# State-space decay matrix from one row-spreading matmul per head and a clamped difference on ScalarE, in place of matmuls of products that POOL made

## The chip, the cores and the metric

The kernel runs on one core of one Trainium2 chip. The metric is device time in microseconds (us): the median of three runs, 1414.44 us before the change (1413.89 to 1421.01). Five engines work side by side, each through its own queue in program order: TensorE (PE in the profile, with its weight loads as PEld), VectorE (DVE), ScalarE (ACT), GpSimd (POOL) and SyncE (SP, which issues most transfers).

## What is computed

The reference is one layer of a hybrid network over 512 tokens of width 1024: an adaptive layer norm, three branches (attention, pooling, a state-space mixer), their gated sum, and a mixture of experts. The change touches the state-space branch alone, which has 32 heads in 4 groups. Cut to what matters:

```python
def ssd_mixer(z, xbc, dt_raw, ...):
    dt = jax.nn.softplus(dt_raw + dt_bias)            # per token and head
    a_cs = jnp.cumsum(dt * a, axis=2)                 # a < 0: running sum in a block
    seg = a_cs[:, :, :, None] - a_cs[:, :, None, :]   # difference of two tokens
    decay = jnp.where(causal, jnp.exp(jnp.where(causal, seg, 0.0)), 0.0)
    cb = jnp.einsum('bclgn,bcsgn->bclsg', cm, bm)     # per group, shared by its 8 heads
    scores = cb[..., None] * decay * dt[:, :, None]
    y_diag = jnp.einsum('bclsgr,bcsgrp->bclgrp', scores, xs)
    states = jnp.einsum('bcsgn,bcsgr,bcsgrp->bcgrpn', bm, decay_end * dt, xs)
    ...                                               # states carried from block to block
    y = y_diag + y_off + d_skip * xs
    y = y * jax.nn.silu(z)                            # then a group norm and w_ssm_o
```

Both kernels use blocks of 128 tokens, so 4 blocks (b = 0 to 3) for the 512 tokens.

## The kernel before

Weights are streamed from memory as 1 MB tiles. Each is split into a high and a low part of a faster matmul type (`whi` by a cast on ScalarE, line 84; the rest by a subtraction on VectorE, line 85, in place of the raw tile), and every product is made of three matmuls (lines 103 to 105, `mm3`). Through most of the kernel these matmuls fill TensorE.

The state-space branch (`ssd_branch`) takes its four groups g = 0 to 3 one after the other. `ssd_proj` makes a group's inputs by projection: x (two weight tiles, moving tiles 512 wide), B and C (`bmt`, `cmt`, one weight tile), then z (two weight tiles, eight result tiles `zs` of 24 matmuls, 256 wide). Each z tile leaves PSUM by a tanh on ScalarE (`zt`, line 463) and a product on VectorE (line 464); projections have four PSUM buffers (tag `mm`), so z tile 6 needs the buffer of z tile 2. Everything else shares four PSUM buffers of the tag `aux`.

`ssd_group` then goes through the 4 blocks. In each it makes C·B (line 480), which VectorE masks into `cbm` (line 482). In two halves of four heads POOL makes the products `rh` and `rl` of the lower triangle with a head's step (line 492), two matmuls with a strict triangle turn these into sums of steps between two tokens (lines 495 and 496), ScalarE takes the exponential (`sc`, line 498), VectorE multiplies with `cbm` (line 499), and only then can TensorE multiply the four heads' scores with the inputs `xdt` (line 502). `rh`, `rl` and `xdt` have one buffer each. Between blocks the state `st` is carried (lines 513 to 522). `ssm_out` (lines 545 to 556) projects the group before back to the model width with `yh` and `yl`; these matmuls, or the next group's, are what TensorE has between the steps of `ssd_group`. `decays` (lines 366 to 416) prepares the steps once, in group 0.

The order of instructions on each engine is made when the program is built: a scheduler places each instruction by program order as priority and by its own estimates of time. On the chip an engine takes its queue strictly in that order, and waits on semaphores for the others.

Of the kernel before, what the change touches and what calls it, by code (L numbers as in the profile page):

```python
# [30 lines left out]
C_ID, C_SEL, C_REC, C_KEY, C_G4, C_IE, C_IOB, C_PU, C_SGN, C_TA, C_TB, C_SLOT, C_K = 0, 128, 144, 208, 224, 228, 244, 251, 257, 258, 262, 266, 394  # L31
C_TRI, C_STR, C_BEF, C_MASK, C_N = 394, 522, 650, 778, 906
S_C, S_BADA, S_B48, S_ALOG, S_DSK, S_CW, S_CB, S_NW, S_PS, S_BR, S_N = 0, 8, 56, 57, 89, 121, 217, 241, 257, 265, 281
# [22 lines left out]
class Net:  # L56
# [88 lines left out]

    # ---------------------------------------------------------------- whole
    def build(self):
# [28 lines left out]
    def consts(self):  # L176
        nc, K = self.nc, self.K
        c = self.c = K.tile([P, C_K], F32, name="consts")
        e = self.ce = self.C.tile([P, C_N - C_K], F32, name="early")
        s = self.s = K.tile([P, S_N], F32, name="small")  # L180
        self.ident = c[:, C_ID:C_ID + P]
        self.tri, self.strict, self.before, self.mask = (e[:, i * P:(i + 1) * P] for i in range(4))
        self.mhalf = K.tile([P, NB], F32, name="mhalf")
# [9 lines left out]
    def copies(self):  # L193
        nc, K, c = self.nc, self.K, self.c
        self.ident_b = K.tile([P, P], BF16, name="ident_b")
        nc.vector.tensor_copy(self.ident_b, self.ident)
        self.mask_b = K.tile([P, P], BF16, name="mask_b")
        nc.vector.tensor_copy(self.mask_b, self.mask)
        self.ones_b = K.tile([P, P], BF16, name="ones_b")
        nc.vector.tensor_copy(self.ones_b, self.ones)  # L200
        self.bef_b = K.tile([P, P], BF16, name="bef_b")
        nc.vector.tensor_copy(self.bef_b, self.before)
        self.strict_r = self.C.tile([P, P], F32R, name="strict_r")
        nc.scalar.copy(self.strict_r, self.strict)
# [159 lines left out]

    # ---------------------------------------------------------------- dt, f
    def decays(self):
        nc, T, K, s, pz = self.nc, self.T, self.K, self.s, self.pz
        v = nc.vector
        n = NB * 48
        t = [T.tile([P, 512], F32, name=nm, tag=nm, bufs=1) for nm in ("y", "yo")]  # L370
        z, a = t[0][:, :n], t[0][:, n:2 * n]
# [45 lines left out]

    # ---------------------------------------------------------------- SSD
    def conv(self, ps, cc, out):
# [9 lines left out]
    def ssd_proj(self, g):  # L429
# [17 lines left out]
        wt = self.weights(self.I["wu"][5 * g + 2])  # L447
        bmt = T.tile([P, S], F32, name="bmt", tag="bmt", bufs=2)
        cmt = T.tile([P, S], F32, name="cmt", tag="cmt", bufs=2)
# [5 lines left out]
        bmn = T.tile([P, S], F32, name="bmn", tag="bmn", bufs=1)  # L455
        nc.scalar.activation(bmn, pt, AF.Copy, scale=0.5)
        zs = T.tile([P, NB, 512], F32, name="zs", tag="zs", bufs=1)
        for u in range(2):
            wt = self.weights(self.I["wu"][5 * g + 3 + u])
            for b in range(NB):  # L460
# [4 lines left out]
                                               op0=OP.add, op1=OP.mult)  # L465
        return xsn, bmt, cmt, bmn, zs

    def ssd_group(self, g, xsn, bmt, cmt, bmn, zs):
        nc, T, s = self.nc, self.T, self.s
# [7 lines left out]
        for b in range(NB):  # L477
            tb = slice(b * P, (b + 1) * P)
            pc = self.aux_tile()
            nc.tensor.matmul(pc[:, :P], bmt[:, tb], cmt[:, tb], start=True, stop=True)  # L480
            cbm = T.tile([P, P], F32, name="cbm", tag="cbm", bufs=2)
            v.tensor_tensor(cbm, pc[:, :P], self.tri4, OP.mult)
            xdt = T.tile([P, 512], F32, name="xdt", tag="xdt", bufs=1)
            v.tensor_tensor(h8(xdt[:, :]), h8(xsn[:, b]), b8(self.sp[:, b, 16 + g * 8:24 + g * 8]), OP.mult)
            py = self.aux_tile()
            for q in range(2):
                h4 = slice(g * 8 + q * 4, g * 8 + q * 4 + 4)
                tb4 = self.tri[:, None, :].to_broadcast([P, 4, P])
                rs = []
                for nm, src in (("rh", self.dah.bitcast(F32)), ("rl", self.dal)):  # L490
                    r = T.tile([P, 4, P], F32R, name=nm, tag=nm, bufs=1)
                    nc.gpsimd.tensor_tensor(r, tb4, src[:, b, h4][:, :, None].to_broadcast([P, 4, P]), OP.mult)  # L492
                    rs.append(r)
                pe = self.aux_tile()
# [8 lines left out]
            y = T.tile([P, 512], F32, name="y", tag="y", bufs=1)  # L503
            nc.gpsimd.tensor_tensor(h8(y[:, :]), h8(xsn[:, b]), b8(s[:, S_DSK + g * 8:S_DSK + g * 8 + 8]), OP.mult)  # L504
            v.tensor_tensor(y, py, y, OP.add)
            if b:
                po = self.aux_tile()
                nc.tensor.matmul(po, cmt[:, tb], state, start=True, stop=True)
                yo = T.tile([P, 512], F32, name="yo", tag="yo", bufs=1)
                v.tensor_tensor(h8(yo[:, :]), h8(po[:, :]), b8(self.ex[:, 0, b, hs]), OP.mult)  # L510
                v.tensor_tensor(y, y, yo, OP.add)
            if b < NB - 1:
                v.tensor_tensor(h8(xdt[:, :]), h8(xsn[:, b]), b8(self.dtd[:, b, hs]), OP.mult)
                pst = self.aux_tile()
                nc.tensor.matmul(pst, bmn[:, tb], xdt, start=True, stop=True)
# [6 lines left out]
                state = new  # L522
            v.tensor_tensor(yg[:, b], y, zs[:, b], OP.mult)
            nc.scalar.activation(y, yg[:, b], AF.Square, accum_out=ssq[:, b:b + 1])
# [61 lines left out]

    # ---------------------------------------------------------------- pool
    def pool_branch(self):
# [46 lines left out]

    # ---------------------------------------------------------------- attention
    def att_branch(self):
# [995 lines left out]
def _layout(inp):  # L1633
# [9 lines left out]
    c[:, C_BEF:C_BEF + P] = n[:, None] < n[None]  # L1643
    c[:, C_MASK:C_MASK + P] = np.where(n[None] > n[:, None], BIG, 0.0)
    c[:, C_SEL:C_SEL + H] = (n[:, None] % 32) == np.arange(H)[None]
    for i, w in enumerate((2, 4, 8, 16)):
# [83 lines left out]
```

## Time and profile before

| | before |
|---|---|
| device time, median of 3 (range) | 1414.44 us (1413.89 to 1421.01) |
| span of the profiled execution | 1413.1 us |
| mean granted TensorE clock | 0.958 |
| PE busy | 1299.2 us, 92% |
| PE weight loads busy | 1059.9 us, 75% |
| VectorE busy | 1075.4 us, 76% |
| ScalarE busy | 651.5 us, 46% |
| POOL busy | 394.3 us, 28% |

The page tells of one profiled execution, whose span is 1.3 us below the median of the timed runs. A busy share is an average over the whole kernel. A matmul's listed time is longer than its step, since matmuls are pipelined: what one costs in a full queue is the distance between two starts. The four groups of the state-space branch lie between 60 us and 480 us. In the tables by stretch, "PEclk" is the clock that the chip granted to TensorE: 1.00 is its upper level (2.4 GHz), 0.50 its lower (1.2 GHz).

### The profile page before, as it was taken

To read this page: it belongs to the slowest core of one execution; us is meant where nothing else is said; L and a number is where in the kernel's file an instruction comes from. 1 tells how busy PE (TensorE), PEld (TensorE's weight loads), DVE (VectorE), ACT (ScalarE), POOL (GpSimd) and SP (SyncE) were. 2 spreads that over 40 slices of the span, in tenths; PEclk is the share of its full clock that TensorE was granted. 3 is DMA by queue.
4 is the path that set the end of the run, shared out by engine and by line. 5 is a ranking of instruction groups with operands and counts; after the bars stand their busy time and mean duration, and the time that the engine had idled before them with its cause. 6 is when DMAs were issued, how large, how long until landed. Compare 5 with 4: busy or idle time off the path is not lost. (4 is left out here: it accounts for less than half of the span.)

```text
span 1413.1 us, 18254 instructions
## 1 busy us (share of the span) xinstructions
PE 1299.2 (92%) x6796; PEld 1059.9 (75%) x6796; DVE 1075.4 (76%) x1643; ACT 651.5 (46%) x1055; POOL 394.3 (28%) x282
## 2 busy tenths in 40 slices
PE   6999998998998999999999999999489899999992
PEld 4797786796796788889877778887367777777771
DVE  7777857658758448794388885676989999999866
ACT  3453432432432323333366665321157876776642
POOL 4415225015015000000112111134524434533442
PEclk7999999999999999999999999999589999999996
DMA  8421120220220227745211013355578998989141
GB/s 325 174 90 60 33 87 30 90 90 30 90 90 30 89 91 296 269 179 210 90 61 59 32 61 121 113 209 215 180 278 306 341 361 283 332 315 360 72 162 61
DMA packets 38635, 224.84 MB, mean 159 GB/s; under 512 B 6275, under 2 KB 6819, under 8 KB 14352
## 3 DMA queue, kind: packets, MB, share of 16 engines
q1 hardware_dynamic: 31008, 208.52, 40.5%
q0 software_dynamic: 4896, 8.85, 1.8%
q10 hardware_dynamic: 2640, 6.29, 1.2%
q8 instruction: 54, 0.88, 0.2%
q14 instruction: 37, 0.30, 0.1%
HBM read 216.35 MB, written 16.27 MB: 165 GB/s over the span
## 5 line engine op out<-in xcount | busy, mean ns | idle before, releaser
L85 DVE TENSOR_TENSOR raw<-raw,whi 128x1024 fp32r<-128x1024 f32 x296 | 371.5, 1278 | 127.2 <-ACT whi L84 117.9
L84 ACT CAST whi<-raw 128x1024 fp32r<-128x1024 f32 x320 | 324.8, 1051 | 186.2 <-PE mm L104 95.0
L103 PE MATMUL mm<-ht,whi 128*128 128x512 f32 x576 | 231.5, 402 | 0.0
L105 PE MATMUL mm<-ht,raw 128*128 128x512 f32 x576 | 229.4, 398 | 0.0
L104 PE MATMUL mm<-ht,whi 128*128 128x512 f32 x576 | 228.3, 396 | 0.0
L103 PE MATMUL mm<-whi,ht 128*128 128x256 f32 (+1 forms) x448 | 133.8, 300 | 0.0
L105 PE MATMUL mm<-whi,ht 128*128 128x256 f32 (+1 forms) x448 | 133.8, 299 | 0.0
L104 PE MATMUL mm<-raw,ht 128*128 128x256 f32 (+1 forms) x448 | 133.7, 299 | 0.0
L105 PEld LDWEIGHTS mm<-ht,raw 128*128 128x128 f32 x576 | 109.1, 189 | 22.4 <-issue 0.8
L103 PEld LDWEIGHTS mm<-ht,whi 128*128 128x128 f32 x576 | 109.5, 190 | 21.1 <-issue 1.0
L104 PEld LDWEIGHTS mm<-ht,whi 128*128 128x128 f32 x576 | 109.4, 190 | 20.8 <-issue 0.5
L104 PE MATMUL mm<-raw,xh 128*128 128x512 f32 x256 | 106.7, 417 | 15.0 <-DVE raw L85 12.7
L103 PE MATMUL mm<-whi,xh 128*128 128x512 f32 x256 | 106.3, 415 | 0.0
L105 PE MATMUL mm<-whi,xl 128*128 128x512 f32 x256 | 104.4, 409 | 1.3 <-DVE xl L85 1.3
L104 PEld LDWEIGHTS mm<-raw,ht 128*128 128x128 f32 x448 | 85.7, 191 | 2.6
L105 PEld LDWEIGHTS mm<-whi,ht 128*128 128x128 f32 x448 | 85.7, 191 | 2.4
L103 PEld LDWEIGHTS mm<-whi,ht 128*128 128x128 f32 x448 | 85.5, 191 | 2.6
L1313 POOL TENSOR_TENSOR yb<-yb,gf 128x512 f32<-128x512 f32 x30 | 43.2, 1441 | 147.4 <-ACT yb L1312 147.3
L85 POOL TENSOR_TENSOR raw<-raw,whi 128x1024 fp32r<-128x1024 f32 x24 | 71.6, 2988 | 36.7 <-ACT whi L84 19.2
L492 POOL TENSOR_TENSOR rh<-early,dah 128x512 fp32r<-128x512 f32 x32 | 36.4, 1138 | 143.3 <-PE aux L495 143.3
L104 PEld LDWEIGHTS mm<-raw,xh 128*128 128x128 f32 x256 | 50.7, 198 | 32.4 <-DVE raw L85 18.1
L504 POOL TENSOR_TENSOR y<-xsn,small 128x512 f32<-128x512 f32 x16 | 26.5, 1655 | 123.1 <-ACT xsn L443 78.4
(431 smaller groups left out, 2726.1 us busy)
## 6 DMA issues: line engine op xcount, KB each, us to landing
raw<-in_we_dram SPq DMA_DIRECT2D x96, 1024.0 KB, 6.8
raw<-in_wu_dram SPq DMA_DIRECT2D x48, 1024.0 KB, 4.9
ra<-in_wada_dram SPq DMA_DIRECT2D x24, 1024.0 KB, 7.0
raw<-in_wso_dram SPq DMA_DIRECT2D x8, 1024.0 KB, 4.9
x<-in_x_dram SPq DMA_DIRECT2D x8, 512.0 KB, 8.4
y_d<-zero ACTq DMA_DIRECT2D x1, 4096.0 KB, 17.2
raw<-in_wao_dram SPq DMA_DIRECT2D x4, 1024.0 KB, 5.0
raw<-in_wout_dram SPq DMA_DIRECT2D x4, 1024.0 KB, 5.0
```

The lines of the kernel that those rows point to most:

```text
L84: h = self.nc.scalar.copy(hi, src)
L85: self.cut = [h, (eng or self.nc.vector).tensor_tensor(lo, src, hi.bitcast(F32), OP.subtract)]
L103: mm(ps, lh, rh, start=first, stop=False)
L104: mm(ps, lh, rl, start=False, stop=False)
L105: self.last_mm = mm(ps, ll, rh, start=False, stop=last)
L492: nc.gpsimd.tensor_tensor(r, tb4, src[:, b, h4][:, :, None].to_broadcast([P, 4, P]), OP.mult)
L504: nc.gpsimd.tensor_tensor(h8(y[:, :]), h8(xsn[:, b]), b8(s[:, S_DSK + g * 8:S_DSK + g * 8 + 8]), OP.mult)
L1313: nc.gpsimd.tensor_tensor(y[:, cs], y[:, cs], self.gf[:, cs], OP.mult)
```

## The change

The running sum `acs` of the steps, which `decays` already had in PSUM for another use, is kept and transposed: `ar` holds it with heads in rows and all 512 tokens in columns, high part in rows 0 to 31 and the rest in rows 32 to 63. For each head a matmul with a 0/1 matrix `pick` copies the head's row to all 128 partitions, for all four blocks at once. ScalarE then takes Relu(acs of the row's token − spread value), block by block (four instructions of 128x128, line 491 of the new file), which is zero above the diagonal, and Exp of its negative over all 512 columns (line 492). VectorE multiplies with `cbm`, now one tile for four blocks (line 493). The scores of a group's 8 heads are made in a new function `ssd_scores`, which `ssd_proj` calls ahead of the z projection; they are kept in 8 buffers (`gt2`, a tag that exists already for the gates). `ssd_group` only uses them. The products of lines 492, 495 and 496 are gone, `xdt` and `y` have two buffers, and the state's input has a tile of its own (`xde`).

```diff
@@ decays
-        self.dah = self.C.tile([P, NB, 32], F32R, name="dah")
-        self.dal = self.C.tile([P, NB, 32], F32, name="dal")
-        nc.scalar.copy(self.dah, da)
-        v.tensor_tensor(self.dal, da, self.dah.bitcast(F32), OP.subtract)
...
+        self.acs = self.C.tile([P, NB, 32], F32, name="acs")
+        nc.scalar.copy(self.acs[:, :, :].rearrange("p b c -> p (b c)"), ps[:, :P])
+        pr = self.aux_tile()
+        for b in range(NB):
+            nc.tensor.transpose(pr[:32, b * P:(b + 1) * P], self.acs[:, b], self.ident)
+        ar = self.ar = self.C.tile([64, S], F32R, name="ar")
+        nc.scalar.copy(ar[:32], pr[:32])
+        v.tensor_tensor(ar[32:], pr[:32], ar[:32].bitcast(F32), OP.subtract)
@@ ssd_proj
+        sc = self.ssd_scores(g, bmt, cmt)
         zs = T.tile([P, NB, 512], F32, name="zs", tag="zs", bufs=1)
@@ new
+    def ssd_scores(self, g, bmt, cmt):
+        nc, T = self.nc, self.T
+        v = nc.vector
+        pc = self.aux_tile()
+        for b in range(NB):
+            tb = slice(b * P, (b + 1) * P)
+            nc.tensor.matmul(pc[:, tb], bmt[:, tb], cmt[:, tb], start=True, stop=True)
+        cbm = T.tile([P, NB, P], F32, name="cbm", tag="cbm", bufs=1)
+        v.tensor_tensor(cbm, pc[:, :].rearrange("p (b c) -> p b c", b=NB), self.tri4[:, None, :].to_broadcast([P, NB, P]), OP.mult)
+        out = []
+        for h in range(8):
+            if h % 4 == 0:
+                pick = T.tile([64, 4, P], F32R, name="pick", tag="pick", bufs=1)
+                nc.gpsimd.tensor_copy(pick, self.heads[:, g * 8 + h:g * 8 + h + 4][:, :, None].to_broadcast([64, 4, P]))
+            pe = self.aux_tile()
+            nc.tensor.matmul(pe, pick[:, h % 4], self.ar, start=True, stop=True)
+            sc = T.tile([P, S], F32, name="sc", tag="gt2", bufs=8)
+            for b in range(NB):
+                tb = slice(b * P, (b + 1) * P)
+                nc.scalar.activation(sc[:, tb], pe[:, tb], AF.Relu, scale=-1.0, bias=self.acs[:, b, g * 8 + h:g * 8 + h + 1])
+            nc.scalar.activation(sc, sc, AF.Exp, scale=-1.0)
+            v.tensor_tensor(sc, sc, cbm[:, :, :].rearrange("p b c -> p (b c)"), OP.mult)
+            out.append(sc)
+        return out
@@ ssd_group
-            xdt = T.tile([P, 512], F32, name="xdt", tag="xdt", bufs=1)
+            xdt = T.tile([P, 512], F32, name="xdt", tag="xdt", bufs=2)
             v.tensor_tensor(h8(xdt[:, :]), h8(xsn[:, b]), b8(self.sp[:, b, 16 + g * 8:24 + g * 8]), OP.mult)
             py = self.aux_tile()
-            for q in range(2):
...
-                for nm, src in (("rh", self.dah.bitcast(F32)), ("rl", self.dal)):
-                    r = T.tile([P, 4, P], F32R, name=nm, tag=nm, bufs=1)
-                    nc.gpsimd.tensor_tensor(r, tb4, src[:, b, h4][:, :, None].to_broadcast([P, 4, P]), OP.mult)
...
-                nc.tensor.matmul(pe, self.strict_r, rs[0][:, :, :].rearrange("p a b -> p (a b)"), start=True, stop=False)
-                nc.tensor.matmul(pe, self.strict_r, rs[1][:, :, :].rearrange("p a b -> p (a b)"), start=False, stop=True)
-                sc = T.tile([P, 4, P], F32, name="sc", tag="sc", bufs=2)
-                nc.scalar.activation(sc[:, :, :].rearrange("p a b -> p (a b)"), pe, AF.Exp)
-                v.tensor_tensor(sc, sc, cbm[:, None, :].to_broadcast([P, 4, P]), OP.mult)
-                for r in range(4):
-                    hc = slice((q * 4 + r) * 64, (q * 4 + r + 1) * 64)
-                    nc.tensor.matmul(py[:, hc], sc[:, r], xdt[:, hc], start=True, stop=True)
+            for h in range(8):
+                hc = slice(h * 64, (h + 1) * 64)
+                nc.tensor.matmul(py[:, hc], sc[h][:, tb], xdt[:, hc], start=True, stop=True)
```

The change moves instructions on three engines. TensorE in group 1 before, one block of `ssd_group`: `mm<-yh,...` are matmuls of the projection back, and `x4` or `x8` merges equal rows in a row.

```order
L480 MATMUL aux<-cmt,bmt 128x128
L495 MATMUL aux<-rh,strict_r 128x512
L496 MATMUL aux<-rl,strict_r 128x512
L103 MATMUL mm<-yh,whi 128x512
...
L105 MATMUL mm<-yh,raw 128x512
L502 MATMUL aux<-xdt,sc 128x64 x4
L495 MATMUL aux<-rh,strict_r 128x512
L496 MATMUL aux<-rl,strict_r 128x512
```

The same engine and group after the change, first where the scores are made (`mm<-whi,ht` 256 wide are matmuls of z), then where a block uses them.

```order
L478 MATMUL aux<-cmt,bmt 128x128 x4
L487 MATMUL aux<-ar,pick 128x512 x3
L103 MATMUL mm<-whi,ht_86 128x256
L104 MATMUL mm<-raw,ht_86 128x256
L487 MATMUL aux<-ar,pick 128x512
...
L513 MATMUL aux<-xdt,sc 128x64 x5
L523 MATMUL aux<-xde,bmn 128x512
L513 MATMUL aux<-xdt,sc 128x64 x8
```

The eight spreading matmuls now lie among the z matmuls, with 2, 6, 8, 11 and 11 of these between the third and the eighth and 52 behind it; the score products of `ssd_group` stand 8 in a row with no step of another engine between them.

TensorE in group 0 after the change, at the last of the eight spreading matmuls:

```order
L104 MATMUL mm<-raw,ht_88 128x256
L105 MATMUL mm<-whi,ht_88 128x256
L487 MATMUL aux<-ar,pick 128x512
L513 MATMUL aux<-xdt,sc 128x64 x5
L523 MATMUL aux<-xde,bmn 128x512
L513 MATMUL aux<-xdt,sc 128x64 x9
L103 MATMUL mm<-whi,ht_85 128x256
```

Here the score products of blocks 0 and 1 follow directly behind the last spreading matmul, ahead of the 96 matmuls of z's second weight tile; before, 139 matmuls of z stood in one piece ahead of block 0.

ScalarE in group 0 after the change, at the end of the eight heads (`zt` is the tanh of z, `whi` the cast of a weight tile, here z's second):

```order
L491 ACTIVATE sc<-aux,acs 128x128 x4
L492 ACTIVATE sc<-sc 128x512
L491 ACTIVATE sc<-aux,acs 128x128 x3
L467 ACTIVATE zt<-mm 128x256
L492 ACTIVATE sc<-sc 128x512
L467 ACTIVATE zt<-mm 128x256 x2
L529 COPY st<-aux 128x512
L84 CAST whi<-raw 128x1024
```

The 32 Relu and 8 Exp instructions of a group stand in one run with nothing else in it until the last head; the cast of z's second weight tile stands behind them, where before it stood behind four `zt`.

## Rows read from the trace of the kernel before

**Rows 1.** Page, 40 slices of the span: busy tenths and granted clock.

```profile
PE   6999998998998999999999999999489899999992
PEclk7999999999999999999999999999589999999996
```

**Rows 2.** Stretches, one per group: length, busy of PE, PEld, DVE, ACT, POOL, PEclk.

```profile
110.00:170.00 60.00, 53.45 (x262) 40.80 (x262) 50.26 (x66) 20.69 (x35) 27.19 (x20) 0.97 0.16 53
200.00:250.00 50.00, 43.44 (x203) 31.89 (x202) 36.16 (x46) 16.91 (x31) 27.04 (x20) 0.97 0.14 48
310.00:370.00 60.00, 53.65 (x251) 40.42 (x250) 49.21 (x64) 17.15 (x29) 25.90 (x20) 0.97 0.15 53
420.00:470.00 50.00, 43.72 (x207) 32.26 (x205) 41.19 (x53) 13.05 (x23) 23.60 (x18) 1.00 0.17 62
```

**Rows 3.** Waits of PE, 90 to 545 us: total us, times, longest us.

```profile
PE aux L502 <- DVE sc L499: 23.0, 20, 1.9
PE aux L144 <- DVE zs L533: 2.7, 4, 0.9
```

**Rows 4.** A stretch of 4 us in group 0, same columns.

```profile
152.00:156.00 4.00, 4.00 (x12) 2.61 (x12) 3.47 (x5) 0.60 (x1) 2.85 (x2) 0.57 0.00 0
```

**Rows 5.** Timeline of PE in group 2: start, length, instruction, idle before it.

```profile
320.15 0.48 PE L495 MATMUL aux<-rh,strict_r 128*128 128x512 f32 x1
...
320.70 0.39 PE L105 MATMUL mm<-yh,raw 128*128 128x512 f32 x1
...
323.86 1.10 PE L502 MATMUL aux<-xdt,sc 128*128 128x64 f32 x8 [1.15 <-DVE sc L499]
324.77 0.48 PE L495 MATMUL aux<-rh,strict_r 128*128 128x512 f32 x1
```

**Rows 6.** Line 499: ns min/median/max, first and last start.

```profile
L499 DVE TENSOR_TENSOR sc<-sc,cbm x32: 691/1523/1556, 114.1 to 461.1; 128x512 f32<-128x512 f32 x32
```

**Rows 7.** Groups of ACT by form: busy us, mean ns, idle before.

```profile
L806 ACT ACTIVATE l<-aux,mn 128x128 f32<-128x128 f32 x16 | 5.9, 369 | 5.2 <-DVE mn L804 5.2
L426 ACT ACTIVATE xst<-cacc 128x512 f32<-128x512 f32 x16 | 10.1, 631 | 16.4 <-DVE cacc L425 16.2
L498 ACT ACTIVATE sc<-aux 128x512 f32<-128x512 f32 x32 | 19.1, 598 | 66.3 <-PE aux L496 58.3 <-DVE st L519 7.6
```

**Rows 8.** Timeline of ACT: small activations in a row, and a cast and what follows.

```profile
33.38 0.41 ACT L272 ACTIVATE mod<-aux,bias 128x1 f32<-128x1 f32 x2 [0.97 <-PE aux L270]
...
905.08 0.90 ACT L674 ACTIVATE ht<-merged 128x128 fp32r<-128x128 f32 x4
```

**Rows 9.** Timeline of PE and DVE at the start of group 3's z projection.

```profile
395.28 0.63 PE L144 MATMUL aux<-consts,bmt 128*128 128x128 f32 x4
395.67 0.36 PE L103 MATMUL mm<-whi,ht 128*128 128x256 f32 x1
...
398.02 0.28 PE L104 MATMUL mm<-raw,ht 128*128 128x256 f32 x1
398.14 0.28 PE L105 MATMUL mm<-whi,ht 128*128 128x256 f32 x1
...
398.79 1.22 DVE L85 TENSOR_TENSOR raw<-raw,whi 128x1024 fp32r<-128x1024 f32 x1
...
401.43 0.69 DVE L427 SCALAR_TENSOR_TENSOR cmt<-cmt,cacc 128x512 f32<-128x512 f32 x1 [0.43 <-ACT cmt L426]
```

**Rows 10.** Timeline of PE: `decays` in group 0, state in group 2.

```profile
91.93 0.28 PE L411 MATMUL aux<-early,sp 128*16 128x128 f32 x1
...
319.12 1.05 PE L515 MATMUL aux<-xdt,bmn 128*128 128x512 f32 x2
320.01 0.39 PE L480 MATMUL aux<-cmt,bmt 128*128 128x128 f32 x2
```

**Rows 11.** Groups by form: POOL copies of 64x512, ACT weight casts.

```profile
L762 POOL CAST q<-consts 64x512 fp32r<-64x512 f32 x16 | 10.2, 634 | 169.9 <-PE mm L104 169.1
L84 ACT CAST whi<-raw 128x1024 fp32r<-128x1024 f32 x320 | 324.8, 1051 | 186.2 <-PE mm L104 95.0 <-PE mm L105 62.1 <-POOL raw L899 10.8
```

More of the change, by code (lines that the diff above doesn't have):

```diff
@@ L31 @@
 C_ID, C_SEL, C_REC, C_KEY, C_G4, C_IE, C_IOB, C_PU, C_SGN, C_TA, C_TB, C_SLOT, C_K = 0, 128, 144, 208, 224, 228, 244, 251, 257, 258, 262, 266, 394
-C_TRI, C_STR, C_BEF, C_MASK, C_N = 394, 522, 650, 778, 906
+C_TRI, C_STR, C_BEF, C_MASK, C_DD, C_N = 394, 522, 650, 778, 906, 938
 S_C, S_BADA, S_B48, S_ALOG, S_DSK, S_CW, S_CB, S_NW, S_PS, S_BR, S_N = 0, 8, 56, 57, 89, 121, 217, 241, 257, 265, 281
@@ L182, in consts @@
         self.tri, self.strict, self.before, self.mask = (e[:, i * P:(i + 1) * P] for i in range(4))
+        self.heads = e[:64, 4 * P:4 * P + 32]
         self.mhalf = K.tile([P, NB], F32, name="mhalf")
@@ L202, in copies @@
         nc.vector.tensor_copy(self.bef_b, self.before)
-        self.strict_r = self.C.tile([P, P], F32R, name="strict_r")
-        nc.scalar.copy(self.strict_r, self.strict)
         self.tri4 = self.C.tile([P, P], F32, name="tri4")
@@ L369, in decays @@
         n = NB * 48
-        t = [T.tile([P, 512], F32, name=nm, tag=nm, bufs=1) for nm in ("y", "yo")]
+        t = [T.tile([P, 512], F32, name=nm, tag=nm, bufs=1) for nm in ("xde", "yo")]
         z, a = t[0][:, :n], t[0][:, n:2 * n]
@@ L447, in ssd_proj @@
         wt = self.weights(self.I["wu"][5 * g + 2])
-        bmt = T.tile([P, S], F32, name="bmt", tag="bmt", bufs=2)
+        bmt = T.tile([P, S], F32, name="bmt", tag="bmt", bufs=1)
         cmt = T.tile([P, S], F32, name="cmt", tag="cmt", bufs=2)
@@ L465, in ssd_proj, with ssd_group @@
                                                op0=OP.add, op1=OP.mult)
-        return xsn, bmt, cmt, bmn, zs
-    def ssd_group(self, g, xsn, bmt, cmt, bmn, zs):
+        return xsn, sc, cmt, bmn, zs
+    def ssd_scores(self, g, bmt, cmt):
[22 more added lines that the diff above has]
+        return out
+    def ssd_group(self, g, xsn, sc, cmt, bmn, zs):
         nc, T, s = self.nc, self.T, self.s
@@ L478, in ssd_group @@
             tb = slice(b * P, (b + 1) * P)
[L479 to L482, printed above, removed]
-            xdt = T.tile([P, 512], F32, name="xdt", tag="xdt", bufs=1)
+            xdt = T.tile([P, 512], F32, name="xdt", tag="xdt", bufs=2)
             v.tensor_tensor(h8(xdt[:, :]), h8(xsn[:, b]), b8(self.sp[:, b, 16 + g * 8:24 + g * 8]), OP.mult)
             py = self.aux_tile()
-            for q in range(2):
-                h4 = slice(g * 8 + q * 4, g * 8 + q * 4 + 4)
-                tb4 = self.tri[:, None, :].to_broadcast([P, 4, P])
-                rs = []
-                for nm, src in (("rh", self.dah.bitcast(F32)), ("rl", self.dal)):
-                    r = T.tile([P, 4, P], F32R, name=nm, tag=nm, bufs=1)
-                    nc.gpsimd.tensor_tensor(r, tb4, src[:, b, h4][:, :, None].to_broadcast([P, 4, P]), OP.mult)
-                    rs.append(r)
-                pe = self.aux_tile()
-                nc.tensor.matmul(pe, self.strict_r, rs[0][:, :, :].rearrange("p a b -> p (a b)"), start=True, stop=False)
-                nc.tensor.matmul(pe, self.strict_r, rs[1][:, :, :].rearrange("p a b -> p (a b)"), start=False, stop=True)
-                sc = T.tile([P, 4, P], F32, name="sc", tag="sc", bufs=2)
-                nc.scalar.activation(sc[:, :, :].rearrange("p a b -> p (a b)"), pe, AF.Exp)
-                v.tensor_tensor(sc, sc, cbm[:, None, :].to_broadcast([P, 4, P]), OP.mult)
-                for r in range(4):
-                    hc = slice((q * 4 + r) * 64, (q * 4 + r + 1) * 64)
-                    nc.tensor.matmul(py[:, hc], sc[:, r], xdt[:, hc], start=True, stop=True)
-            y = T.tile([P, 512], F32, name="y", tag="y", bufs=1)
+            for h in range(8):
+                hc = slice(h * 64, (h + 1) * 64)
+                nc.tensor.matmul(py[:, hc], sc[h][:, tb], xdt[:, hc], start=True, stop=True)
+            y = T.tile([P, 512], F32, name="y", tag="y", bufs=2)
             nc.gpsimd.tensor_tensor(h8(y[:, :]), h8(xsn[:, b]), b8(s[:, S_DSK + g * 8:S_DSK + g * 8 + 8]), OP.mult)
-            v.tensor_tensor(y, py, y, OP.add)
             if b:
@@ L508, in ssd_group @@
                 nc.tensor.matmul(po, cmt[:, tb], state, start=True, stop=True)
-                yo = T.tile([P, 512], F32, name="yo", tag="yo", bufs=1)
-                v.tensor_tensor(h8(yo[:, :]), h8(po[:, :]), b8(self.ex[:, 0, b, hs]), OP.mult)
-                v.tensor_tensor(y, y, yo, OP.add)
             if b < NB - 1:
-                v.tensor_tensor(h8(xdt[:, :]), h8(xsn[:, b]), b8(self.dtd[:, b, hs]), OP.mult)
+                xde = T.tile([P, 512], F32, name="xde", tag="xde", bufs=1)
+                v.tensor_tensor(h8(xde[:, :]), h8(xsn[:, b]), b8(self.dtd[:, b, hs]), OP.mult)
                 pst = self.aux_tile()
-                nc.tensor.matmul(pst, bmn[:, tb], xdt, start=True, stop=True)
+                nc.tensor.matmul(pst, bmn[:, tb], xde, start=True, stop=True)
                 new = T.tile([P, 512], F32, name="st", tag="st", bufs=2)
@@ L522, in ssd_group @@
                 state = new
+            v.tensor_tensor(y, py, y, OP.add)
+            if b:
+                yo = T.tile([P, 512], F32, name="yo", tag="yo", bufs=1)
+                v.tensor_tensor(h8(yo[:, :]), h8(po[:, :]), b8(self.ex[:, 0, b, hs]), OP.mult)
+                v.tensor_tensor(y, y, yo, OP.add)
             v.tensor_tensor(yg[:, b], y, zs[:, b], OP.mult)
@@ L1644, in _layout @@
     c[:, C_MASK:C_MASK + P] = np.where(n[None] > n[:, None], BIG, 0.0)
+    c[:, C_DD:C_DD + 32] = (n[:, None] % 32) == np.arange(32)[None]
     c[:, C_SEL:C_SEL + H] = (n[:, None] % 32) == np.arange(H)[None]
```

## The prediction

> **What bounds the kernel now.** I read the page's slices first. PE is busy nine tenths or more in nearly every one, and one of the dents comes with a lower clock [rows 1]. So time is lost or won where PE stands still or does needless work. I then cut the state-space branch into stretches, one around each group's `ssd_group`: in the four, PE is busy 53.45 of 60, 43.44 of 50, 53.65 of 60 and 43.72 of 50 us [rows 2], so it stands still 6.55 + 6.56 + 6.35 + 6.28 = 25.7 us. The waits of PE name the cause: 23.0 us in 20 waits of the score product (line 502) for VectorE's multiplication (line 499), and 2.7 us in 4 waits of the transposes behind the group norm [rows 3]. The scores come too late because POOL, PE, ScalarE and VectorE hand each half block on in turn, while the order has only some 3 to 13 projection matmuls to put between. VectorE's step is itself slow there: 1523 ns in the median against 691 ns at best [rows 6]. Last, the clock: behind the waits (up to 1.9 us each [rows 3]) a stretch of 4 us has a mean clock of 0.57, PE being busy throughout [rows 4]; group 1 and group 2 have one such stretch each, which is why their PEclk reads 0.97 as well, and group 3 has none [rows 2].
>
> **What goes.**
> (1) The 25.7 us of standing still, if the scores lie ready.
> (2) A wait costs more than its idle time shows, since PE's last matmul counts as busy for its listed 0.39 us while the next of a full queue would start after about 0.23 us. That is 0.16 us for each of the 24 waits [rows 3, 5]: 3.8 us. (0.23 us is the step of the wide matmuls; the pair below confirms it.)
> (3) The clock: 3 stretches x 4 us x 0.43 lost [rows 4] = 5.2 us.
> (4) The pairs of lines 495 and 496: from 320.15 to 320.70 is 0.55 us for a pair [rows 5], and there are 32 [rows 6] = 17.6 us. In their place stand 32 single matmuls of the same 512 columns, at half a pair each, 8.8 us. Saved 8.8 us. They use 64 rows of the array instead of 128; should that change the step, the bounds are 0.23 and 0.32 us each, 7.4 to 10.2 us in all.
> Sum 25.7 + 3.8 + 5.2 + 8.8 = 43.5 us.
>
> POOL's 64 products vanish and eight small copies (`pick`) come; a copy of 64x512 takes 634 ns [rows 11]. POOL is no bound either way, but the fifth head's matmul waits for the group's second copy, which can start only after the fourth head's: 0.6 us, against the 6 z matmuls between the two (0.72 us). VectorE's multiplications no longer meet POOL and should fall from 1523 towards 691 ns; that changes no term, since PE has z matmuls meanwhile. The score products themselves (8 listed instructions, four heads, 0.91 us [rows 5]), the state matmuls (0.89 us [rows 10]) and C·B stay.
>
> **What comes.** The new work is on ScalarE: per head four Relu of 128x128 from PSUM with a per-partition bias, and one Exp of 128x512. The trace has no such Relu. Its nearest row is line 806, the same shape from PSUM with a bias: 369 ns [rows 7]. But ScalarE overlaps neighbours: two 128x1 activations listed at 0.26 us each take 0.41 us together, and four of 128x128 without bias take 0.90 us, a step of about 0.2 [rows 8]. I take 369 less the same 0.1 us, 0.27 us, with 0.2 and 0.37 as ends. The Exp: 631 ns for such a shape from SBUF [rows 7], so 0.53 us as a step, 0.63 as an end. A head is 4 x 0.27 + 0.53 = 1.6 us (1.3 to 2.1), eight are 12.8 us, with nothing else between them in the queue. Over the kernel that is 51 us in place of 19.1 us for line 498 [rows 7], on an engine that is half idle.
>
> What that has to fit into, in groups 1 to 3: PE reaches z tile 6 after 90 z matmuls of 0.12 us [rows 9] and eight spreading matmuls, 10.8 + 2.2 = 13 us after the first spreading matmul, plus 0.7 us of score products. Tile 6 needs tile 2's buffer, whose tanh stands behind the last Relu: 0.5 us for the first matmul, 12.3 us of chain up to that Relu, 0.4 us each for tanh and product, 13.6 us. It just fits. The buffers of the sixth to eighth spreading matmul come free within a few tenths of the time at which PE gets there. The other input, `cmt`, is finished at 402.1 us in group 3, and PE, from 395.67 us on, gets through the 54 z matmuls ahead of C·B at 402.2 us [rows 9]: level, and VectorE now has two more multiplications ahead of it. I allow 1.0 us of new waits a group, 3.0 us for three. Further on, eight score products in a row (1.8 us) and two or more projection matmuls cover the copy and addition of the state, and 77 projection matmuls instead of 11 to 19 cover the norm ahead of the transposes.
>
> Group 0 is different. The sums of `decays` end at 91.93 us [rows 10]; copy, transposes, cast and subtraction of `ar` lie beside matmuls that are there anyway, so only the four transposes count, at the 0.1 us of those at 395.28 [rows 9]: 0.4 us. The first spreading matmul comes near 97 us. Up to the last one PE has 36 z matmuls and its eight, 6.5 us; then the score products stand directly behind. ScalarE needs 12.8 us, VectorE's last multiplication 0.7 us. PE can use some of the gap, since early heads are ready and a state matmul lies between, but waits 5 us. Then z's second weight tile: its cast (1.05 us [rows 11]) and subtraction (1.22 us [rows 9]) are queued behind the eight heads, and 96 z matmuls wait for them, about 1.5 us more. Together 6.5 us, and one more lapse of the clock, 1.7 us, as behind the shorter waits of before: 8.2 us. With half the work ahead (1.3 us a head) the wait would be 4 us; at 2.1 us, 10.5 us.
>
> Sum of what comes: 3.0 + 0.4 + 8.2 = 11.6 us. Net 43.5 - 11.6 = 31.9 us. The profiled execution's span is 1413.1 us, so 1381.2; it lies 1.3 us below the median of the runs, and the forecast is 1382.5 us, written 1383. Behind the branch the order on every engine is the same as before, and transfers start when buffers come free, so the lead should last to the end.
>
> One page speaks against the step on ScalarE: the Trainium skill, "ScalarE: Activation LUTs", "Rules for kernel authors", wants relu on VectorE and budgets about 0.3 us per ACTIVATE with a pointer bias plus 0.83 ns per element. By it a head would be 4 x 0.41 + 0.73 = 2.35 us, an estimate from that page, and the sum would come to about 1409 us. The rows differ from it where activations follow each other (0.90 us for four).
>
> **Rivals.**
> A. ScalarE does not overlap these instructions (each Exp waits for its four Relu, and writes in place). A head costs 4 x 0.37 + 0.63 = 2.1 us; 0.5 us more for eight heads in four groups is 16 us, taken by PE at the reused buffers, at tile 6 and at group 0's score products. 1399 us; with a clock lapse in each of the other three groups 1404. For it: the dependence, and that the fit is level. Against it: the next head's first Relu stands between, and the overlaps in [rows 8]. The page's rule above is this rival with a larger price.
> B. Slower: ScalarE becomes the bound. The point is found from the sum: 31.9 us less one lapse (1.7 us) in three groups leaves 26.8 us, over 32 heads 0.84 us, so from 2.4 us a head, a Relu step of 0.47 us, nothing is left, and at 0.55 us (2.7 a head) it is some 10 us slower, 1424 us. No row of that shape reaches 0.47 us; longer waits at reused buffers could add lapses.
> C. The lead is given back later: a stage behind it already waits for transfers that don't start earlier. Half of it would be left, 1398 us. Against it: PE is as busy there as here [rows 1], and between 90 and 545 us PE's waits hold none for a transfer.
>
> **How the numbers follow.** Chances: forecast 0.77, A 0.13, B 0.04, C 0.06. The forecast's own range is 1372 (no new waits: 43.5 less the transposes) to 1393 us (2.1 us a head in group 0 and 3 us of waits in each other group). The range, 1371 to 1404, takes in A and C and leaves out B and the worst of A. What a measurement of this kernel can tell from no change is about 0.5%, 7 us: faster by more 0.92, within 0.04, slower 0.04.
>
> **What would show it.** Right: PE has next to no idle in the four stretches but for some 5 us before the score products of group 0; PEclk 1.00 in groups 1 to 3; Relu starts 0.27 us apart; groups 1 to 3 shorter by 8 to 10 us each and group 0 by 2 to 4 us. Wrong: waits of a spreading matmul for Relu, or of z tile 6 for its buffer, of several us in every group (A, B); a state-space branch that ends 30 us earlier while the end moves less (C).

## The result, and the profile after

The changed kernel takes 1382.51 us in the median of 4 runs (1379.47 to 1384.13), the kernel before 1417.49 us (1413.89 to 1421.01, 4 runs): a ratio of 0.9754, with a 95% interval of 0.9730 to 0.9779. Forecast were 1383 us and faster. The profiled execution took 1384.13 us, with a span of 1382.4 us. The total was right; two of its terms were wrong by about 8 us each, in opposite directions. One execution of an experiment below (1494.84 us, where the nine others of its kernel took 1418.60 to 1427.01 us) was in a slow state and is left out of the times.

TensorE and its clock in the 40 slices, which answer to [rows 1]:

```profile
PE   6999999999999999999999999998489899999992
PEclk7899999999999999999999999999589999999996
```

The dents of the state-space branch are gone. The four stretches of [rows 2], moved to where the same work now lies (length, busy of PE and its count, PEclk, DMA share, GB/s):

```profile
105.00:165.00 60.00, 59.86 (x352) 1.00 0.21 71
192.00:242.00 50.00, 50.00 (x276) 1.00 0.18 64
295.00:355.00 60.00, 59.99 (x314) 1.00 0.21 71
397.00:447.00 50.00, 50.00 (x267) 1.00 0.19 64
```

25.7 us of standing still have become 0.15 us, and the clock is 1.00 in all four: the three lapses are gone and no new one came. From the first sum of `decays` to the pool branch PE stands still 3.8 us in all, nearly all of it outside these stretches. The waits of PE, 60 to 545 us, which answer to [rows 3] (total us, times, longest):

```profile
PE aux L144 <- DVE bmt L430: 3.4, 3, 1.4
PE mm L103 <- DVE cacc L428: 0.5, 1, 0.5
PE aux L487 <- POOL pick L485: 0.2, 1, 0.2
```

There is no wait for a score, for Relu or for a z buffer. The largest wait is new: in groups 2 and 3 VectorE does two multiplications of `ssd_group` ahead of the last step of `bmt` (`xdt` at 267.81 and `xde` at 268.42, then `bmt` at 269.88), where before there was one (`xdt` at 283.25, then `bmt` at 284.06), and PE's transposes of `bmt` stand still for it. ScalarE in group 0, timeline (start, length, instruction):

```profile
104.76 1.22 ACT L491 ACTIVATE sc<-aux,acs 128x128 f32<-128x128 f32 x4
105.75 0.74 ACT L492 ACTIVATE sc<-sc 128x512 f32<-128x512 f32 x1
106.29 1.24 ACT L491 ACTIVATE sc<-aux,acs 128x128 f32<-128x128 f32 x4
```

From 104.76 to 106.29 a head takes 1.53 us: four Relu in 0.99 us, 0.25 us apart, and an Exp of 0.54 us. That is the forecast's 1.6 us (0.27 and 0.53). The sums of the groups show what became of the score steps beside it (busy us, mean ns; the second answers to [rows 6]):

```profile
L492 ACT ACTIVATE sc<-sc 128x512 f32<-128x512 f32 x32 | 23.2, 724 | 0.0
L493 DVE TENSOR_TENSOR sc<-sc,cbm 128x512 f32<-128x512 f32 x32 | 22.1, 692 | 26.4 <-ACT sc L492 26.1
```

The Exp is listed at 724 ns but steps at 0.54 us, so a listed length is no pace where instructions follow each other. VectorE's multiplication went from 1523 ns in the median to 692 ns, as forecast, now that POOL's products are gone; in the experiment below that keeps these products it takes 1475 ns.

**Where the time went.** The groups are measured from one `bmt` transpose to the next, the last one to the pool branch's first copy. Before (group 3 starts at 395.28 [rows 9]):

```profile
175.25 0.28 PE L103 MATMUL mm<-whi,ht 128*128 128x256 f32 x1
...
178.18 0.66 PE L144 MATMUL aux<-consts,bmt 128*128 128x128 f32 x4
...
285.55 0.63 PE L144 MATMUL aux<-consts,bmt 128*128 128x128 f32 x4
...
540.14 0.59 ACT L607 COPY pa<-mm 128x512 f32<-128x512 f32 x1 [3.69 <-PE mm L105]
```

After:

```profile
93.52 0.61 PE L397 MATMUL aux<-yo,early 128*128 128x128 f32 x4
...
170.04 0.66 PE L144 MATMUL aux<-consts,bmt 128*128 128x128 f32 x4 [0.60 <-DVE bmt L430]
...
271.56 0.63 PE L144 MATMUL aux<-consts,bmt 128*128 128x128 f32 x4 [1.41 <-DVE bmt L430]
...
373.00 0.63 PE L144 MATMUL aux<-consts,bmt 128*128 128x128 f32 x4 [1.41 <-DVE bmt L430]
...
509.58 0.59 ACT L620 COPY pa<-mm 128x512 f32<-128x512 f32 x1 [3.69 <-PE mm L105]
```

Group 0 is counted from the first sum of `decays`, 93.52 us here and 91.17 us before.

| | before | after | saved | forecast |
|---|---|---|---|---|
| group 0 | 87.0 | 76.5 | 10.5 | 2 to 4 |
| group 1 | 107.4 | 101.5 | 5.9 | 8 to 10 |
| group 2 | 109.7 | 101.4 | 8.3 | 8 to 10 |
| group 3 | 144.9 | 136.6 | 8.3 | 8 to 10 |

The border between groups 0 and 1 is not the same in the two kernels: before, 24 z matmuls of group 1 (2.9 us, from 175.25) stand ahead of its `bmt` transposes and count for group 0, after the change they stand behind. For the same matmuls group 0 saved 7.6 us and group 1 8.8 us, so groups 1 to 3 came out as forecast and group 0 did not.

Together 32.9 us; `decays` begins 2.35 us later, which leaves 30.6 us at the pool branch, and 30.7 us at the end (1413.1 against 1382.4). From the pool branch on nothing is given back.

### The profile page after: what moved, and what is told of

It reads as the page before. It is cut to its first block, busy times and chain, and to the rows that moved or that the text cites. A ratio compares the mean times of both kernels' runs of the same rounds, so it can differ in the third digit from the quotient of the medians.

```text
span 1382.4 us, 18259 instructions
## 1 busy us (share of the span) xinstructions
PE 1292.2 (93%) x6768; PEld 1059.2 (77%) x6768; DVE 1043.1 (75%) x1631; ACT 682.6 (49%) x1183; POOL 308.7 (22%) x226
## 5 line engine op out<-in xcount | busy, mean ns | idle before, releaser
L103 PE MATMUL mm<-whi,ht 128*128 128x256 f32 (+1 forms) x448 | 135.6, 303 | 0.6 <-DVE cacc L428 0.5
L105 PE MATMUL mm<-whi,ht 128*128 128x256 f32 (+1 forms) x448 | 135.4, 302 | 0.0
L515 POOL TENSOR_TENSOR y<-xsn,small 128x512 f32<-128x512 f32 x16 | 19.8, 1246 | 227.1 <-ACT xsn L446 139.0
L105 PEld LDWEIGHTS mm<-whi,xl 128*128 128x128 f32 x256 | 50.5, 197 | 12.6 <-DVE xl L85 2.0
```

The costliest lines, as they stand in the source:

```text
L103: mm(ps, lh, rh, start=first, stop=False)
L105: self.last_mm = mm(ps, ll, rh, start=False, stop=last)
```

## Experiments

Ratios are to the kernel before on the same chip, with their 95% intervals. The changed kernel, run again beside the first three, gives the base: 1382.97 us, 0.9759 (0.9737 to 0.9782).

> The changed kernel once more, unaltered, as the base for the runs beside it: 1382 us, ratio to before 0.973 to 0.978.

### The spreading matmul with 128 rows

The timeline of PE in the changed kernel, group 1, showed where a listed-busy PE lost time (start, listed length):

```profile
180.45 0.28 PE L104 MATMUL mm<-raw,ht 128*128 128x256 f32 x1
180.66 0.49 PE L487 MATMUL aux<-ar,pick 64*128 64x512 f32 x1
...
181.30 0.28 PE L103 MATMUL mm<-whi,ht 128*128 128x256 f32 x1
```

z matmuls start 0.12 us apart, but from 180.45 to 181.30, with one spreading matmul between two of them, it is 0.85 us. The edit:

```
-self.heads = e[:64, 4 * P:4 * P + 32]
+self.heads = e[:, 4 * P:4 * P + 32]
-ar = self.ar = self.C.tile([64, S], F32R, name="ar")
+ar = self.ar = self.C.tile([P, S], F32R, name="ar")
+v.memset(ar[64:].bitcast(F32), 0.0)
-pick = T.tile([64, 4, P], F32R, ...)
+pick = T.tile([P, 4, P], F32R, ...)
```

> The spreading matmuls use 128 rows (64 of them zeros) instead of 64; the order of TensorE's queue is the same. Theory (changing between 128-row and 64-row weights costs TensorE time that is listed as busy): in the trace after, two z matmuls with a spreading matmul between them start 180.45 and 181.30, 0.85 us for what should be 0.12 + 0.21 + 0.12; 0.40 us a run of 64-row matmuls, 25 such runs (7 in group 0, 6 in each other), so 10 us less: 1372 us, about 0.993 of the changed kernel, and a spreading matmul's step of 0.21 us. Rival 1 (the extra time is a short wait for an aux buffer, for pick or for the weight load, which shows nowhere): no change, 1382 us, the step stays. Rival 2 (a 64-row matmul of 512 columns is itself slow): also 10 us less, but then the three in a row at 178.00 would have cost 0.6 us each, and they take 0.90 us together.

Measured: 1376.31 us, 0.9722 (0.9697 to 0.9748), 6.7 us less than the base in the medians. The same place in its trace:

```profile
182.67 0.28 PE L103 MATMUL mm<-whi,ht 128*128 128x256 f32 x1
182.79 0.40 PE L488 MATMUL aux<-ar,pick 128*128 128x512 f32 x1
...
183.14 0.28 PE L105 MATMUL mm<-whi,ht 128*128 128x256 f32 x1
```

The same stretch takes 0.47 us (182.67 to 183.14) instead of 0.85: changing from 128 rows to 64 and back costs 0.38 us, and no row calls it a wait. It is the change that costs and not the matmul: the three spreading matmuls in a row at the head of the group, from the C·B ahead of them to the second z matmul behind them, take 2.11 us with 64 rows (177.01 to 179.12) and 1.71 us with 128 (178.43 to 180.14), 0.40 us for all three together. The intervals of the two ratios just overlap, so the verdict rests on the steps and on the groups, from one `bmt` transpose to the next. With 128 rows:

```profile
171.46 0.66 PE L144 MATMUL aux<-consts,bmt 128*128 128x128 f32 x4 [0.61 <-DVE bmt L431]
...
271.11 0.63 PE L144 MATMUL aux<-consts,bmt 128*128 128x128 f32 x4 [1.42 <-DVE bmt L431]
```

That is 99.65 us for group 1, where the base has 101.50 (171.19 to 272.69), and group 2 has 99.61 against 101.51. That makes 1.9 us a group and 0.31 us for each of 6 runs, not 0.40: two of the six now take a tenth or two longer than the others. One of them, at 181.50, starts 0.30 us behind its predecessor, right behind POOL's second `pick` copy of the group (180.84 to 181.45); what holds the other is not shown. In group 0, counted from its own `bmt` transposes as in all that follows, hardly anything is gained (71.93 us against 72.16), because there PE now waits 1.65 us in three places, two of them shown (PE, and ScalarE's Relu of the fifth head):

```profile
107.70 1.24 ACT L492 ACTIVATE sc<-aux,acs 128x128 f32<-128x128 f32 x4
...
108.74 1.10 PE L514 MATMUL aux<-xdt,sc 128*128 128x64 f32 x8 [1.05 <-ACT sc L492]
110.24 0.43 PE L514 MATMUL aux<-xdt,sc 128*128 128x64 f32 x2 [0.40 <-DVE sc L494]
```

The first is no wait for a score, since a score comes from VectorE (line 494). The score products of the first block write one of the four `aux` buffers, which go round; it is the one that the fifth head's spreading matmul filled, and it is free when that head's Relu has read it: the four Relu begin at 107.70, the Exp behind them at 108.72, PE goes on at 108.74. Only the other 0.6 us are waits for scores.

So the theory holds, at 6.7 us instead of 10; rival 1 would have left the step as it was.

### The old method, made early

The products of POOL and the pairs of matmuls of before, made ahead of z into eight kept buffers; the core of the edit in `ssd_scores`:

```
for b in range(NB):
    for q in range(2):
        ...
        nc.gpsimd.tensor_tensor(r, tb4, src[:, b, h4]..., OP.mult)   # rh, rl
        ...
        nc.tensor.matmul(pe, self.strict_r, rs[0]..., start=True, stop=False)
        nc.tensor.matmul(pe, self.strict_r, rs[1]..., start=False, stop=True)
        sc = T.tile([P, 4, P], F32, name="sc", tag="gt2", bufs=8)
        nc.scalar.activation(sc..., pe, AF.Exp)
        v.tensor_tensor(sc, sc, cbm[:, b]..., OP.mult)
```

> Placement alone: the method of before (64 products on POOL, pairs of matmuls, one Exp a half block) but made ahead of the z projection into eight kept buffers, with the loop over blocks as in the changed kernel (y with one buffer, since the room ends). Theory (the placement would have taken the waits away only if POOL could keep up): the order puts 5 to 6 z matmuls, 0.7 us, and a pair, 0.5 us, between half blocks, and POOL needs 2.1 to 2.7 us for its two products: TensorE waits for POOL some 7 x 1.0 to 1.5 us a group, 28 to 42 us in all, in place of the 25.7 us of before: 1405 to 1430 us. Rival (the gain is that the scores lie ready, whatever makes them): 1382 + 8.8 us for the pairs = 1391 us.

Measured: 1421.15 us in the median of nine, 1.0047 (1.0028 to 1.0066): the placement alone is no gain. POOL's timeline in group 1, and the waits of PE, 60 to 560 us:

```profile
187.74 1.03 POOL L486 TENSOR_TENSOR rh<-early,dah 128x512 fp32r<-128x512 f32 x1
188.74 1.03 POOL L486 TENSOR_TENSOR rl<-early,dal 128x512 fp32r<-128x512 f32 x1
189.74 1.48 POOL L486 TENSOR_TENSOR rh<-early,dah 128x512 fp32r<-128x512 f32 x1
191.19 1.48 POOL L486 TENSOR_TENSOR rl<-early,dal 128x512 fp32r<-128x512 f32 x1
```

```profile
PE aux L489 <- POOL rh L486: 8.0, 26, 0.7
PE aux L490 <- POOL rl L486: 5.4, 9, 1.0
```

POOL works without a gap at 2.0 to 2.9 us a half block and sets the pace. The waits are shorter than I expected (13.4 us, not 28 to 42), but there are 35 of them, and the clock pays: it is 0.88 in 90 to 160 us, 0.95 in 160 to 270, and 0.94 in 270 to 380 and in 380 to 520, where the base has 1.00 in all four. That is an estimated 29 us (12% of 70, 5% of 110, 6% of 110 and of 140 us), more than the waits themselves.

In the kernel before it was the other way round. There PE waits for POOL nowhere [rows 3], and POOL stands still for PE, whose first matmul of a pair (line 495) frees the one buffer of `rh` (total us, times):

```profile
  PE aux L495: 143.3, 27
```

So POOL's products were not the pace of the old kernel. They became it when all eight half blocks of a group were made in one go; the waits for a late score (line 499 before) are gone in this run too.

### The new method, at the old place

```
 ssd_proj:   -sc = self.ssd_scores(g, bmt, cmt)
 ssd_group:  +sc = self.ssd_scores(g, bmt, cmt)    # first statement, behind the z projection
```

> Method alone: the spreading matmul, Relu and Exp of the changed kernel, but the eight scores of a group are made at the head of the loop over blocks, behind the z projection. Theory (both halves of the change are needed): from the first spreading matmul to the last score ScalarE needs 8 x 1.54 us + 1.5 us = 13.8 us, and the order holds about 10.5 us of work for TensorE in that stretch: 3 to 4 us of waits a group, 12 to 16 us, with up to 5 us of lapses of the clock: 1394 to 1403 us. Rival (the method alone carries the gain, since 1.54 us a head for all four blocks is short enough wherever it stands): 1382 to 1386 us.

Measured: 1385.54 us, 0.9796 (0.9756 to 0.9837); the interval overlaps the base's, and the rival was right. My theory failed because I counted the filler at 0.12 us a matmul. The order takes others (timeline of PE, group 2):

```profile
305.29 0.50 PE L486 MATMUL aux<-ar,pick 64*128 64x512 f32 x1
305.72 0.50 PE L103 MATMUL mm<-yh,whi 128*128 128x512 f32 x1
...
307.31 0.50 PE L486 MATMUL aux<-ar,pick 64*128 64x512 f32 x1
```

The output projection of the previous group (`ssm_out`, 0.23 us each) stands between the heads, 2.02 us from one spreading matmul to the next, enough for ScalarE's 1.54 us, and no PE wait for a score is left anywhere. Group 0 takes 77.8 us, group 1 99.8 us (176.55 to 276.37) and group 2 101.8 us. Here too 24 z matmuls of group 1 (2.9 us) stand ahead of the border; for the same matmuls it is 74.9 us against 72.2 in group 0, 102.7 against 101.5 in group 1, 101.8 against 101.5 in group 2. Group 0, which has no previous group, pays most, by one wait: PE stands still for the low part of one of the next group's weight tiles, and not for a tile of z, whose matmuls are 256 wide.

```profile
153.45 0.50 PE L105 MATMUL mm<-ht,raw 128*128 128x512 f32 x1 [2.90 <-DVE raw L85]
```

So the method carries the gain at either place. Two things at least changed with it, one pass a head for all four blocks and a VectorE multiplication that no longer stands beside POOL's products (1523 ns before, 691 ns here); which of them ended the waits for scores, no run separates.

### More work on ScalarE

```
+nc.scalar.activation(sc, sc, AF.Relu)   # once, or twice
 nc.scalar.activation(sc, sc, AF.Exp, scale=-1.0)
```

> ScalarE gets one more pass over each head's differences (a Relu in place, which changes nothing), some 0.52 us a head: 2.06 us instead of 1.54, the price of rival A. The order moves the last spreading matmuls of a group 10 to 12 z matmuls further back. Theory (ScalarE has slack in groups 1 to 3 and little in group 0): in group 1 after, the last score is ready near 191.5 us and its product stands near 198 us, so 4.2 us more fit but for the reused z buffers, about 2 us a group; group 0 loses 3.6 us: 8 to 10 us more, 1391 us (1386 to 1397). Rival (the prediction's A: half a microsecond a head is paid in full, 16 us): 1399 us. Rival (the order hides it all): 1383 us.

> Two more such passes, 2.6 us a head, beyond the 2.4 us at which the prediction's rival B saw the whole gain used up. Theory (slack of 4 to 6 us a group, then paid in full): 3 x 6.5 + 7.7 = 27 us more, 1410 us (1400 to 1416). Rival B as the prediction sized it: no faster than before, 1414 to 1424 us. Rival (the order spreads the heads out and hides most of it): 1385 to 1395 us.

Measured: one pass 1388.98 us, 0.9831 (0.9798 to 0.9864); two passes 1401.24 us, 0.9911 (0.9884 to 0.9938). Against the base's 0.9759 these are 10 and 21 us. Both lie in the ranges of my theories, and rival B as sized is refuted, but the place is not where I put it. With one pass groups 1 and 2 take 101.58 and 101.57 us, as in the base: there 0.5 us a head costs nothing. In the two traces, whose spans are 1387.8 and 1381.2 us, all of the difference is in group 0 (79.6 us against 72.2). There PE waits 1.57 us and 0.22 us for Relu to free an `aux` buffer, as in the run with 128 rows, and 0.21 us for a score, and the clock follows (stretches of 4 us, same columns as above):

```profile
108.00:112.00 4.00, 2.41 (x9) 0.69 0.68 250
112.00:116.00 4.00, 3.79 (x13) 0.50 0.01 4
116.00:120.00 4.00, 4.00 (x21) 0.50 0.00 0
120.00:124.00 4.00, 4.00 (x23) 0.60 0.00 0
```

At 4 us each the clock lost here is 4 x (0.31 + 0.50 + 0.50 + 0.40) = 6.8 us, more than three times the waits before it. The run with 128 rows stood still there for 1.50 us from 108 to 116 us, against 1.80 us here, and kept its clock:

```profile
108.00:112.00 4.00, 2.67 (x14) 1.00 0.76 264
```

So a stop of about this length may bring a lapse or not; these runs don't show what decides. With two passes group 1 takes 105.1 and group 2 103.6 us: the slack there is over 4.2 us (8 x 0.52) and under 8.3 us a group.

### The clamp on VectorE

```
-nc.scalar.activation(sc[:, tb], pe[:, tb], AF.Relu, scale=-1.0, bias=self.acs[...])
+v.tensor_scalar(sc[:, tb], pe[:, tb], self.acs[...], 0.0, op0=OP.subtract, op1=OP.min)
-nc.scalar.activation(sc, sc, AF.Exp, scale=-1.0)
+nc.scalar.activation(sc, sc, AF.Exp)
```

> The clamp on VectorE (subtract, then min with 0, four of 128x128 from PSUM a head), Exp alone on ScalarE, as the Trainium skill's page on ScalarE ("ScalarE: Activation LUTs", "Rules for kernel authors") would have it. Theory (ScalarE's 1.54 us a head is not what TensorE waits for, so a faster clamp is worth nothing, and VectorE gets 32 x 0.8 = 26 us more): 1380 to 1388 us. Rival (ScalarE's pace sets the end of each group's scores): 5 us or more faster, under 1378 us. Rival (VectorE is in the way: longer waits of the transposes for bmt and of the chain behind the scores): over 1390 us.

Measured: 1390.23 us, 0.9842 (0.9811 to 0.9872), some 12 us slower than the clamp on ScalarE. My 1380 to 1388 us missed it narrowly. The time of the rival with VectorE in the way (over 1390 us) came, but not by its waits: those for `bmt` are no longer (2.8 us, 3.4 in the base). The reason lies in group 0 again (81.1 us against 72.2); groups 1 to 3 take 101.8, 101.7 and 136.7 us, within 0.3 us of the base. In group 0 (ScalarE, VectorE, PE):

```profile
106.24 1.05 ACT L84 CAST whi<-raw 128x1024 fp32r<-128x1024 f32 x1 [2.92 <-PE mm L105]
...
107.85 0.69 DVE L493 TENSOR_TENSOR sc<-sc,cbm 128x512 f32<-128x512 f32 x1 [2.51 <-ACT sc L492]
...
110.41 2.37 PE L513 MATMUL aux<-xdt,sc 128*128 128x64 f32 x10 [3.55 <-DVE sc L491]
```

The order puts the cast of the next group's weight tile between two Exp. It waits 2.92 us for PE to finish with an older tile, VectorE waits 2.51 us for the Exp behind it, and VectorE's later clamp of the fifth head (line 491) frees PE's `aux` buffer 3.55 us late. The clock is 0.83 from 90 to 130 us, 6.8 us more.

Here the measurement goes against the rule of the Trainium skill, "ScalarE: Activation LUTs", "Rules for kernel authors", that relu belongs on VectorE. Its price for ScalarE, 0.41 us a Relu by the estimate that the prediction made from it, is not what the trace shows either, where they step at 0.25 us. What makes the difference in this kernel is the order of the queues in group 0; in groups 1 to 3 the clamp costs the same on either engine.

### Both engines, and 128 rows

```
 if h % 2 == 0:  Relu on ScalarE, Exp with scale=-1.0
 else:           subtract and min on VectorE, Exp with scale=1.0      # with the 128-row edit
```

> 128-row spreading matmuls, and the clamp of every second head on VectorE. In the run with 128 rows alone TensorE waited 1.6 us in group 0 for scores and some tenths in each group for buffers. Theory (there the pace of ScalarE had become the limit): these go, 2 to 3 us less than with 128 rows alone, 1373 to 1375 us. Rival (VectorE's queue is no shorter than ScalarE's): 1376 to 1380 us.

Measured: 1372.63 us, 0.9708 (0.9686 to 0.9730), the fastest of all. Its interval and the base's don't overlap; by the ratios it is 7 us under the changed kernel, and by the groups too. No wait for a score is left from 60 to 560 us, and of the waits for a buffer that Relu holds one of 0.2 us, by a state matmul (line 527). Group 0 takes 70.7 us (71.9 with 128 rows alone), groups 1 and 2 99.6 us each, as with 128 rows alone. So the 1.6 us of waits went, as my theory had it, but from the run with 128 rows alone it can't be told apart by the times.

## Why the prediction was right, step by step

- **(1), (2) Standing still, 25.7 + 3.8 us.** Right. What did it was the method, and the early place did not by itself. Made early, POOL's products at 2.0 to 2.9 us a half block became the pace, and nothing was gained; with 1.54 us a head for all four blocks even the old place leaves no wait for a score. The prediction did not tell the two apart. The 3.8 us of hidden tails no run measures by itself.
- **(3) The clock, 5.2 us.** Right: 1.00 in all four stretches.
- **(4) The pairs, 8.8 us.** Wrong in size. The step that failed is "They use 64 rows of the array instead of 128; should that change the step, the bounds are 0.23 and 0.32 us each". I bounded the matmul and not the change of shape between neighbours. At 0.23 us for each of 32 and 0.38 us for each of 25 runs of them (7 in group 0, 6 in each other) the new matmuls cost 7.4 + 9.5 = 16.9 us in place of 17.6. Saved were 0.7 us.
- **New waits in groups 1 to 3, 3.0 us.** The size was right (3.4 us) and the place wrong: not the reused buffers but `bmt`, for which VectorE's multiplications of the group before are in the way; I had named them for `cmt` alone. That taking them out of the way would recover it wasn't tried.
- **Group 0, 8.2 us.** Wrong, and the other way: nothing of it came. The step that failed is "then the score products stand directly behind", by which I had PE wait for all eight heads. The timeline of PE there, after:

```profile
107.92 0.49 PE L487 MATMUL aux<-ar,pick 64*128 64x512 f32 x1
108.34 1.33 PE L513 MATMUL aux<-xdt,sc 128*128 128x64 f32 x10
109.50 1.08 PE L523 MATMUL aux<-xde,bmn 128*128 128x512 f32 x2
110.42 2.21 PE L513 MATMUL aux<-xdt,sc 128*128 128x64 f32 x18
...
124.39 0.56 PE L513 MATMUL aux<-xdt,sc 128*128 128x64 f32 x4
```

  Two listed matmuls make one product, so 14 products run up to 112.6 us: seven heads of two blocks. The eighth head's two stand at 124.39, behind the rest of z. Nothing waits for the last head, and the seven come just in time, which the runs above show from the other side: a little faster PE (128 rows) or a little slower ScalarE (one more pass) makes PE wait right here, first for the buffer of the fifth head and then for scores. PE also arrives later than I had it, 8.9 us after the first spreading matmul (99.40 to 108.34) and not 6.5, mostly because of the 64-row changes (seven of them at 0.38 us): the error in (4) paid for part of this one.

  The 1.5 us for z's second weight tile rest on a wrong reading, here and in the text on the change. The cast behind the eight heads is not that tile's. ScalarE in group 0, after:

```profile
88.86 1.04 ACT L84 CAST whi<-raw 128x1024 fp32r<-128x1024 f32 x1
...
113.49 1.18 ACT L84 CAST whi<-raw 128x1024 fp32r<-128x1024 f32 x1
```

  z's second tile is cast at 87.39 and 88.86, ahead of the first head, and its 96 matmuls run from 112.77 on. The cast at 113.49 is that of the next group's first x tile, whose matmuls begin at 126.16. With neither wait there was no lapse of the clock either.
- **ScalarE's 1.6 us a head.** Right, 1.53 us. ScalarE overlaps these instructions, so A's condition did not hold, and its price was wrong too: 0.5 us more a head costs 10 us and not 16, in the trace all of it in group 0. Rival B's point, 2.4 us a head, lies too low: at 2.6 us the kernel is still 0.9% faster than before. Between the two runs 0.52 us a head cost about 11 us; carried on from 0.9911, which is an estimate, nothing is left near 3.2 us. The 1409 us that the prediction gave for 2.35 us a head is 1407 by its own sum (0.75 us more for 32 heads), and the times measured at about 2.06 and 2.6 us a head lie below it.
- **Rival C.** Refuted: 30.6 us at the pool branch, 30.7 us at the end.

By these measured terms 25.7 + 3.8 + 5.2 + 0.7 us went; 3.6 us of waits (`bmt` and `pick`), their hidden tails (4 x 0.16) and 0.4 us of transposes came. The transposes and all tails are the forecast's estimates. That makes 30.8 us, and the groups show 32.9. The 2.1 us between are not placed. Of the 2.35 us by which `decays` starts later, the wait for `cacc` (0.45 us at 91.78, which the kernel before doesn't have) and its tail are 0.6. The rest is not placed either: up to there PE's order is the same in both kernels, the mean clock of the first 60 us is 0.74 in place of 0.80, and over the runs of all kernels it lay between 0.72 and 0.80.

That the total came out within a microsecond is luck to the extent of these two terms. With (4) at 0.7 us the same sum gives 1390.6 us, with group 0 at nothing 1374.3 us; either would still have been faster and within the range of 1371 to 1404 us.

## What to carry to other kernels

A listed-busy TensorE can lose time: compare the starts of neighbouring matmuls with the step of an undisturbed row of the same kind, above all where a matmul with fewer rows stands alone among full ones. Before a wait is forecast, read from the order which instruction really stands behind the late input, and how much of the rest can run without it. Moving a chain of engines earlier helps only if each of its steps keeps up at the new place: POOL's products, for which TensorE waited nowhere before, became what it waited for. And when a matmul waits for an engine that doesn't make its input, ask which buffer that engine still reads.

## What the runs showed of the hardware

- A lone 64-row fp32r matmul of 512 columns among 128-row ones costs 0.38 us more than a 128-row one whose upper rows are zeros (0.85 against 0.47 us), a run of three 0.40 us more for all three, and PE is listed as busy meanwhile.
- Four Relu of 128x128 from PSUM with a per-partition bias step at 0.25 us, though each is listed at 0.44 us in the mean; the same clamp on VectorE is listed at 0.34 us (128 of them, 35.8 us).
- VectorE's product of 128x512 takes 692 ns in the median without POOL's products beside it, 1523 and 1475 ns with them.
- PE stood still 1.80 us from 108 to 116 us in the run with one more pass, and 6.8 us of clock were lost; in the run with 128 rows it was 1.50 us, and none was lost.
